# Giving each gathered block its own PSUM bank, from two pools by turns, and placing half of the shared expert behind the first gather

## The chip, the cores and the metric

The kernel runs on one core of a Trainium2 chip. The metric is the time of one execution on the device, in microseconds (us). Smaller is better. The core has a matrix engine (TensorE, PE in the rows, with its weight loads as PEld), a vector engine (VectorE, DVE), an activation engine (ScalarE, ACT), GpSimd (POOL) and SyncE (SP), which here only issues transfers from memory. [...]

## What is computed

One layer of a diffusion backbone over 256 latent tokens of width 1024. The first half (a recurrence, a neighbourhood attention, projections) is not touched by the change. The second half is a mixture of experts, and the change lies there:

```
scores = sigmoid(xb @ w_router)                      # 64 experts
sel = scores + router_bias                           # 4 of 8 groups, then the 8 best experts
w = scores[best] / sum(scores[best]) * 2.5
gates = sum(one_hot(best) * w)                       # token x expert
a = einsum('td,edf->tef', xb, w_e_gate)
u = einsum('td,edf->tef', xb, w_e_up)
act = silu(a) * u * gates
routed = einsum('tef,efd->td', act, w_e_down)
shared = (silu(xb @ w_sh_gate) * (xb @ w_sh_up)) @ w_sh_down
y2 = routed + shared
```

Each of the 64 experts has 3 MB of weights (gate and up 1 MB each, down 1 MB), read from memory once. The shared expert has the same shape and sees all tokens. Everything is in fp32, with some operands split in a high and a low part.

## The kernel before

**Routing.** After the first half, two tiles of 128 tokens (t = 0 and 1) are normalised, transposed on PE (L1194, from `x2` into tiles `pt`), scaled into `h2`, and multiplied with the router (L1204). `choose(t)` (L1159) finds the eight experts on DVE. Small products and DVE steps (L1222 to L1264) then rank the experts by load and give each token its place in its expert. PE's order in this stretch is not written out by hand: a scheduler at build time lists the instructions by readiness, earlier lines first, and takes the slots of a PSUM tag in the order in which the program asks for them.

**The shared expert.** `shared_gu(t, ks, after)` (L1470) multiplies the tokens of tile t with the shared gate and up weights: 16 matmuls for each t, which the trace counts as 32 records since an fp32 matmul is run in two. They read `h2` and the shared weights only. `after` names a PE instruction behind which the scheduler has to put them.

**Units.** The experts' work is cut into 29 units of up to 128 rows; each unit holds the tokens of one to four experts, in the order of `_ORDER` (L34). From L1488 on PE's order is written out, by `_program` (L53). For each unit u it is:

- `g`: `gate_up(u)` (L1393), the products with gate and up of the unit's experts into a `pgu` tile
- `s`: the first half of `scatter` (L1426) of unit u-1: two `py` products (t = 0 and 1), each added into `y` by DVE (L1432)
- `P`: `places(u+1)` (L1352): two transposes into `poh`, read twice by DVE (L1359, L1361); behind every second one `prepare` makes the one-hot matrix of the next pair of units on DVE
- `t`: `act_t(u)` (L1286): the activation on ACT, the product on DVE (L1294), two transposes `pat` on PE, a copy on ACT
- `S`: the second half of the scatter, two more `py` products
- `G`, in every second unit: `gather` (L1364) for the next pair of units
- `d`: `down(u)` (L1411), two `pdn` products, split by ACT (L1421) and DVE (L1422)

**The gather** makes the transposed tokens of a pair of units: for each of eight blocks k four matmuls (L1375) into PSUM, and then one instruction that scales the block into `xg`: on ACT for even k (L1378), on DVE for odd k (L1381). Blocks k and k+1 share one `pxg` tile, each in its half of the bank. The tool that builds the kernel orders all accesses of a PSUM tile by the bank and not by the bytes. The first gather (L1482) is called once before the units, is 128 columns wide and stands among the matmuls of `shared_gu`; the other fourteen stand in the units and are 256 columns wide.

**PSUM tags** (L1126 to L1136): `gu` has four banks, for `pgu` and for all tiles of `ps_y` (`py` and some of the routing); `mm` has two (`pxg`, `poh`, `pat`, and some of the routing); `dn` has two.

**Weights.** SP issues every load in the program's order (`fetch`, `fetch_ahead`, L258 and L294), each as soon as its slot in SBUF is free. There are six slots for gate and up and seven for down; a slot is freed when the last unit that uses its expert has run `g` or `d`. One of each is held by the shared expert at first. SP is in order, so a load that waits for its slot holds up those behind it.

Of the kernel before, what the change touches and what calls it, by code (L numbers as in the profile page):

```python
# [9 lines left out]
F32 = mybir.dt.float32  # L10
# [7 lines left out]
P = 128  # L18
D = 1024
T = 256  # L20
# [114 lines left out]
def build(ctx, tc, I, out, dbg=None):  # L135
    nc = tc.nc
# [6 lines left out]
    def pool(name, bufs=1, **kw):  # L143
        return ctx.enter_context(tc.tile_pool(name=name, bufs=bufs, **kw))
# [64 lines left out]
    def mpool(name, bufs=1, **kw):  # L209
        return mix.enter_context(tc.tile_pool(name=name, bufs=bufs, **kw))  # L210

    psum = mpool("psum", space=bass.MemoryType.PSUM)
# [902 lines left out]
    psum = pool("psum2", space=bass.MemoryType.PSUM)  # L1115
# [8 lines left out]
    fetch_ahead(False)  # L1124

    def ps_gu():  # L1126
        return psum.tile([P, 512], F32, tag="gu", name="pgu", bufs=4)

    def ps_mm(name):
        return psum.tile([P, 512], F32, tag="mm", name=name, bufs=2)  # L1130
# [1 line left out]
    def ps_dn():  # L1132
        return psum.tile([P, 512], F32, tag="dn", name="pdn", bufs=2)

    def ps_y():
        return psum.tile([P, 512], F32, tag="gu", name="py", bufs=4)  # L1136

    pb_ = route.enter_context(tc.tile_pool(name="pb", bufs=1))

# [3 lines left out]
    x2h = pkeep.tile([P, 2, KD, P], F32R, name="x2h")  # L1143
    x2l = pkeep.tile([P, 2, KD, P], F32R, name="x2l")
    y = x1
# [3 lines left out]
    on_pe, turned = [None, None], [None, None]  # L1149
# [39 lines left out]
    for t in range(2):  # L1189
        ts = slice(t * P, (t + 1) * P)  # L1190
        for kk in (0, 4):
            pt = ps_y() if t else ps_mm("pt")
            for i in range(4):
                turned[t] = nc.tensor.transpose(pt[:, i * P:(i + 1) * P], x2[:, t, kk + i, :], ident)  # L1194
            for i in range(4):
                k = kk + i
                if t and i % 2:
                    nc.vector.tensor_scalar(h2[k][:, ts], pt[:, i * P:(i + 1) * P], mod2[:, 1, k:k + 1],
                                            mod2[:, 0, k:k + 1], op0=OP.mult, op1=OP.add)
                else:  # L1200
                    on_act = nc.scalar.activation(h2[k][:, ts], pt[:, i * P:(i + 1) * P], AF.Identity,
                                                  bias=mod2[:, 0, k:k + 1], scale=mod2[:, 1, k:k + 1])
        for k in range(KD):
            on_pe[t] = nc.tensor.matmul(pl[:, t * NE:(t + 1) * NE], h2[k][:, ts], wr[:, k, :], start=(k == 0),  # L1204
                                        stop=(k == KD - 1))
        choose(t)
# [11 lines left out]


    pcn = ps_y()  # L1220
    for t in range(2):
        nc.tensor.matmul(pcn[:NE, 0:1], mask[:, t, :], ones[:, 0:1], start=(t == 0), stop=(t == 1))  # L1222
    pkr = ps_mm("pkr")
    for t in range(2):
# [14 lines left out]
    nc.vector.scalar_tensor_tensor(place, pp[:, 0:2 * NE].rearrange("p (t e) -> p t e", e=NE), 1.0, mask,  # L1239
                                   op0=OP.add, op1=OP.mult)  # L1240
    pix = ps_y()
    nc.tensor.matmul(pix[0:1, :NE], C("ecol")[:NE], R, start=True, stop=True)
    idx = pkeep.tile([1, NE], I32, name="idx")
# [61 lines left out]
    def prepare(pair):  # L1305

        us = [u for u in (2 * pair - 1, 2 * pair) if 0 <= u < len(units)]
        oh = pb2.tile([P, 2, 2 * P], F32R, tag="oh", name="oh", bufs=1)
        res = []
        for i, u in enumerate(us):  # L1310
            later = []
            used = 32 * sum(s[3] for s in units[u])
            if used < P:
                nc.vector.memset(oh[:, :, i * P + used:(i + 1) * P].bitcast(F32), 0.0)
            segs = list(units[u])
            while segs:
                j, s0, t0, n = segs[0]
                run = 1
                while run < len(segs) and segs[run][0] == j + run and segs[run][3] == n and not s0:
                    run += 1  # L1320
                segs = segs[run:]
                w_ = 32 * n
                a, b = 32 * t0, 32 * t0 + run * w_
                if run > 1:
                    sh4 = [P, 2, run, w_]
                    it = iota[:, None, None, 1:1 + w_].to_broadcast(sh4)
                    f4 = "p t (r c) -> p t r c"
                    nc.vector.tensor_tensor(oh[:, :, i * P + a:i * P + b].rearrange(f4, c=w_), it,
                                            pos[:, :, j:j + run, None].to_broadcast(sh4), op=OP.is_equal)
                else:  # L1330
                    for t in range(2):
                        nc.vector.tensor_scalar(oh[:, t, i * P + a:i * P + b], iota[:, s0 + 1:s0 + 1 + w_],
                                                pos[:, t, j:j + 1], None, op0=OP.is_equal)
                later.append((j, run, w_, a, b))
            res.append((u, i, used, later))
        return oh, res
# [27 lines left out]
    def gather(ohs_):  # L1364

        oh, res = ohs_
        w_ = len(res) * P
        xg = pb2.tile([P, KD, 2 * P], F32, tag="xg", name="xg", bufs=1)
        for k in range(KD):
            if k % 2 == 0:  # L1370
                pair_ = ps_mm("pxg")
            pg_ = pair_[:, k % 2 * T:k % 2 * T + w_]
            for t in range(2):
                for part in (x2h, x2l):
                    nc.tensor.matmul(pg_, part[:, t, k, :], oh[:, t, :w_],  # L1375
                                     start=(t == 0 and part is x2h), stop=(t == 1 and part is x2l))
            if k % 2 == 0:
                nc.scalar.activation(xg[:, k, :w_], pg_, AF.Identity, bias=mod2[:, 0, k:k + 1],  # L1378
                                     scale=mod2[:, 1, k:k + 1])
            else:  # L1380
                nc.vector.tensor_scalar(xg[:, k, :w_], pg_, mod2[:, 1, k:k + 1], mod2[:, 0, k:k + 1],  # L1381
                                        op0=OP.mult, op1=OP.add)
        for u, *_ in res:
            xgs[u] = xg

    def pieces(u):

        w_ = 32 * min(4 if n == 4 else 2 if n == 2 else 1 for *_, n in units[u])
        for j, _, t0, n in units[u]:
            for s in range(32 * t0, 32 * (t0 + n), w_):  # L1390
                yield j, s, w_

    def gate_up(u):  # L1393
        i = prep[u][0]
        xg = xgs.pop(u)
        o = ps_gu()
        for k in range(KD):
            for j, s, w_ in pieces(u):
                nc.tensor.matmul(o[s:s + w_], xg[:, k, i * P + s:i * P + s + w_], W["g"][j][:, :, k, :],  # L1399
                                 start=(k == 0), stop=(k == KD - 1))  # L1400
        return o
# [32 lines left out]
    def scatter_open(n, used, ohs, r_, _):  # L1434

        for t in range(2):
            pys[t, n] = py = ps_gu() if n else ps_y()
            for q, a in enumerate(r_[n]):
                nc.tensor.matmul(py, ohs[:used, t * P:(t + 1) * P], a[:used], start=(q == 0), stop=False,
                                 skip_group_check=True)  # L1440
# [25 lines left out]
    gu, dn = shw  # L1466

    pgs = [ps_gu(), ps_gu()]

    def shared_gu(t, ks, after):  # L1470
        with tc.issue_after(after):
            for k in ks:
                for q in range(2):
                    r = nc.tensor.matmul(pgs[t][:, q * FE:(q + 1) * FE], h2[k][:, t * P:(t + 1) * P], gu[:, q, k, :],  # L1474
                                         start=(k == 0 and q == 0), stop=(k == KD - 1 and q == 1),
                                         skip_group_check=True)
        return r.ins

    shared_gu(0, range(3), turned[0].ins)
    shared_gu(0, range(3, 8), turned[1].ins)  # L1480
    ohs_ = prepare(0)
    gather(ohs_)  # L1482
    shared_gu(1, range(8), on_pe[1].ins)
    free["g"].append(shs[0])
    fetch_ahead()

# [4 lines left out]
    for t in range(2):  # L1491
        for n in range(2):
            ns = slice(n * 512, (n + 1) * 512)
            py = ps_y()
# [6 lines left out]
    ohs_ = prepare(1)  # L1501
# [44 lines left out]
    for op, i in steps:  # L1546
        if op == "G":
            gather(ohs_)
        elif op == "P":
            places(ohg_)  # L1550
            if i % 2 == 0 and i < last_u:
                ohs_ = prepare(i // 2 + 1)
# [58 lines left out]
    with tc.If(nov > 0):  # L1611
# [3 lines left out]
        for k in range(KD):  # L1615
            px = ps_mm("px")
            for t in range(2):
                for part in (x2h, x2l):
                    nc.tensor.matmul(px[:, t * P:(t + 1) * P], part[:, t, k, :].bitcast(F32), ident,
                                     start=(part is x2h), stop=(part is x2l))  # L1620
            nc.vector.tensor_scalar(xa[:, k, :], px[:, :T], mod2[:, 1, k:k + 1], mod2[:, 0, k:k + 1],
                                    op0=OP.mult, op1=OP.add)
        with tc.For_i(0, NE, 1) as jv:
# [6 lines left out]
            for t in range(2):  # L1630
                o = ps_gu()
                for k in range(KD):
                    nc.tensor.matmul(o, xa[:, k, t * P:(t + 1) * P], ge[:, :, k, :], start=(k == 0),
                                     stop=(k == KD - 1))
                at = act_t(o, gl_[:, t, :])
                for n in range(2):
                    pd = ps_dn()
                    for jj in range(2):
                        nc.tensor.matmul(pd, at[:, jj, :], de[:, jj, n * 512:(n + 1) * 512], start=(jj == 0),
                                         stop=(jj == 1))  # L1640
# [34 lines left out]
```

## Time and profile before

| | |
|---|---|
| median of 3 runs | 1171.97 us (1171.61 to 1176.51) |
| the profiled execution: its own time | 1173.35 us |
| its span, first to last instruction | 1171.6 us |
| PE busy in the span | 1060.3 us (91%) |
| DVE busy | 678.0 us (58%) |
| ACT busy | 454.0 us (39%) |
| read from HBM | 293.05 MB |
| mean granted clock of PE | 0.964 |

The rows are of one execution. "Idle before, releaser" is the time that an engine stood still before an instruction, and what it waited for last. A busy PE is not a PE at its peak: ends of matmuls are modelled, so two starts tell more than a start and an end. [...] In the table by stretches the columns are the stretch, its length, busy us and instructions of PE, PEld, DVE, ACT and POOL, PEclk, the mean busy share of the DMA engines, and GB/s.

### The profile page before, as it was taken

The numbers are of one execution on the slowest core, as the hardware profiler recorded it, in microseconds if no ns is written. First come the engines' busy times: TensorE is split into PE (matmuls) and PEld (weight loads), VectorE is DVE, ScalarE is ACT, GpSimd is POOL, SyncE is SP. The second block draws the span as 40 slices with busy tenths as digits, with TensorE's granted clock in tenths as the row PEclk, the third lists the DMA queues.
The fourth block names the chain that finished last, engine by engine and source line by source line (L and its number), as shares of the span: only waits on it lengthen the run. The fifth ranks groups of instructions, "written<-read, shape, count | busy, mean of one in ns | idle before, by whom it ended". The sixth has DMA issues, their size and how long they took to land.

```text
span 1171.6 us, 18971 instructions
## 1 busy us (share of the span) xinstructions
PE 1060.3 (91%) x7232; PEld 744.9 (64%) x7232; DVE 678.0 (58%) x1323; ACT 454.0 (39%) x874; POOL 226.9 (19%) x215
## 2 busy tenths in 40 slices
PE   5998989999999989989988899899999999999995
PEld 3796968879898878779987544344434443444441
DVE  5587696958854868777784234343434434434355
ACT  4585847657644556556432011121111111211120
POOL 1126142343455537330010000000000000000021
PEclk9999989898999999999986989999999999999998
DMA  9945444534594434424975479999999999958991
GB/s 320 287 138 164 126 154 133 161 127 130 159 199 130 105 86 75 94 76 132 375 291 231 149 291 368 404 423 403 372 425 424 423 424 426 423 230 344 427 397 38
DMA packets 115101, 295.36 MB, mean 252 GB/s; under 512 B 7080, under 2 KB 86896, under 8 KB 90432
## 3 DMA queue, kind: packets, MB, share of 16 engines
q1 hardware_dynamic: 113088, 290.46, 65.8%
q0 software_dynamic: 1776, 3.47, 3.2%
q8 instruction: 58, 0.95, 0.3%
q14 instruction: 35, 0.29, 0.1%
q10 hardware_dynamic: 144, 0.20, 0.0%
HBM read 293.05 MB, written 1.05 MB: 251 GB/s over the span
## 4 chain that ended last, share of the span: by engine, by line
PE 53%; DVE 14%; DMA 9%; ACT 8%; issue 8%; POOL 5%; SPq 2%; DVEq 0%; ACTq 0%; POOLq 0%
PE pgu L1399 14%; PE proj L388 10%; PE pdn L1407 7%; PE pxg L1375 5%; PE py L1431 4%; DMA dn<-in_w_e_down_dram 3%; DVE wlo L336 3%; DMA wada<-in_w_ada_dram 2%; ACT xg L1378 2%; DMA G<-in_na_rpb_dram 2%; PE proj L394 2%; PE pgu L1474 1%; POOL kl L957 1%; DVE s L728 1%; DMA gu<-in_w_e_up_dram 1%
## 5 line engine op out<-in xcount | busy, mean ns | idle before, releaser
L1399 PE MATMUL pgu<-gu,xg 128*32 128x512 f32 (+1 forms) x1456 | 206.8, 593 | 3.4 <-DMA gu<-in_w_e_up_dram 1.8
L336 DVE TENSOR_TENSOR wlo<-wraw,whi 128x1024 fp32r<-128x1024 f32 x102 | 143.5, 1408 | 44.1 <-ACT whi L335 42.1
L1399 PEld LDWEIGHTS pgu<-gu,xg 128*32 128x32 f32 (+1 forms) x1456 | 65.4, 117 | 140.5 <-issue 129.2
L335 ACT CAST whi<-wraw 128x1024 fp32r<-128x1024 f32 x102 | 105.6, 1045 | 46.3 <-PE proj L388 35.5
L1294 DVE SCALAR_TENSOR_TENSOR ac<-ac,gcol,pgu 128x256 f32<-128x256 f32 (+1 forms) x29 | 13.9, 480 | 170.2 <-ACT ac L154 170.2
L1407 PE MATMUL pdn<-dn,at 128*32 128x512 f32 (+3 forms) x740 | 107.0, 595 | 0.0
L388 PE MATMUL proj<-hl,whi 128*128 128x256 f32 (+1 forms) x480 | 103.8, 331 | 0.0
L388 PE MATMUL proj<-hh,whi 128*128 128x256 f32 (+1 forms) x480 | 103.0, 333 | 0.0
L1375 PE MATMUL pxg<-oh,x2h 128*128 128x256 f32 (+1 forms) x240 | 68.6, 314 | 37.3 <-ACT xg L1378 36.9
L388 PE MATMUL proj<-hh,wlo 128*128 128x256 f32 (+1 forms) x480 | 101.1, 331 | 0.0
L1513 POOL TENSOR_TENSOR end<-cf,mod 128x1024 f32<-128x1024 f32 x1 | 1.9, 1898 | 497.8 <-DMA dn<-in_w_e_down_dram 497.8
L154 ACT ACTIVATE ac<-pgu 128x256 f32<-128x256 f32 (+1 forms) x31 | 11.9, 385 | 202.2 <-PE pgu L1399 192.3
L388 PEld LDWEIGHTS proj<-hh,wlo 128*128 128x128 f32 x480 | 77.0, 196 | 9.0 <-issue 1.4
L388 PEld LDWEIGHTS proj<-hh,whi 128*128 128x128 f32 x480 | 75.8, 196 | 7.0 <-issue 0.5
L388 PEld LDWEIGHTS proj<-hl,whi 128*128 128x128 f32 x480 | 74.8, 194 | 6.5 <-issue 0.7
L1375 PEld LDWEIGHTS pxg<-oh,x2h 128*128 128x128 f32 x240 | 46.5, 194 | 50.2 <-ACT xg L1378 48.7
L1421 ACT CAST rh<-pdn 128x512 fp32r<-128x512 f32 x56 | 32.8, 586 | 109.7 <-PE pdn L1407 94.8
L1381 DVE TENSOR_SCALAR xg<-pxg,mod 128x256 f32<-128x256 f32 (+1 forms) x60 | 32.0, 535 | 64.2 <-PE pxg L1375 63.5
L1432 DVE TENSOR_TENSOR x<-x,py 128x512 f32<-128x512 f32 x108 | 68.9, 679 | 0.0
L1422 DVE TENSOR_TENSOR rl<-pdn,rh 128x512 fp32r<-128x512 f32 x56 | 38.6, 691 | 51.2 <-ACT rh L1421 51.1
L601 ACT ACTIVATE wada<-wada,cond 128x256 f32<-128x256 f32 x128 | 58.6, 502 | 24.1 <-DMA wada<-in_w_ada_dram 24.1
L1407 PEld LDWEIGHTS pdn<-dn,at 128*32 128x32 f32 (+2 forms) x740 | 29.8, 117 | 58.9 <-issue 56.1
(389 smaller groups left out, 2057.3 us busy)
## 6 DMA issues: line engine op xcount, KB each, us to landing
gu<-in_w_e_gate_dram SPq DMA_DIRECT2D x64, 1024.0 KB, 12.3
gu<-in_w_e_up_dram SPq DMA_DIRECT2D x64, 1024.0 KB, 13.2
dn<-in_w_e_down_dram SPq DMA_DIRECT2D x61, 1024.0 KB, 13.4
wraw<-in_w_in_dram SPq DMA_DIRECT2D x80, 512.0 KB, 4.6
wada<-in_w_ada_dram SPq DMA_DIRECT2D x48, 512.0 KB, 4.6
wraw<-in_w_branch_a_dram SPq DMA_DIRECT2D x8, 512.0 KB, 3.5
wraw<-in_w_branch_b_dram SPq DMA_DIRECT2D x8, 512.0 KB, 3.9
wraw<-in_w_out_dram SPq DMA_DIRECT2D x8, 512.0 KB, 7.7
```

What stands on the lines that cost most here:

```text
L335: nc.scalar.copy(hi, raw)
L336: nc.vector.tensor_sub(lo, raw, hi.bitcast(F32))
L388: nc.tensor.matmul(o, a[:, m * P:(m + 1) * P], b[:, :n], start=first, stop=last)
L601: nc.scalar.activation(w, w, AF.Identity, scale=cond[:, k, 0:1])
L1375: nc.tensor.matmul(pg_, part[:, t, k, :], oh[:, t, :w_], start=(t == 0 and part is x2h), stop=(t == 1 and part is x2l))
L1381: nc.vector.tensor_scalar(xg[:, k, :w_], pg_, mod2[:, 1, k:k + 1], mod2[:, 0, k:k + 1], op0=OP.mult, op1=OP.add)
L1399: nc.tensor.matmul(o[s:s + w_], xg[:, k, i * P + s:i * P + s + w_], W["g"][j][:, :, k, :], start=(k == 0), stop=(k == KD - 1))
L1407: nc.tensor.matmul(pd[s:s + w_, :ns.stop - ns.start], at[:, jj, s:s + w_], W["d"][j][:, jj, ns], start=(jj == 0), stop=(jj == 1))
L1421: nc.scalar.copy(rh[:used], z)
L1422: last_rl[0] = nc.vector.tensor_sub(rl[:used], z, rh[:used].bitcast(F32)).ins
L1431: nc.tensor.matmul(py, ohs[:used, t * P:(t + 1) * P], a[:used], start=(q == 0), stop=(q == 1))
L1432: nc.vector.tensor_add(to[:, t, ns], to[:, t, ns], py)
```

## The change

`ps_y` gets a tag of its own, `y`, with two banks, and `gu` keeps two instead of four. The gather takes a new tile for every block k: k = 0, 1, 4, 5 from `mm` and k = 2, 3, 6, 7 from `y`. `gather` returns its last matmul, and `shared_gu(1, ...)` is put behind that one; before it was put behind the router's last matmul of tile 1.

```diff
     def ps_gu():
-        return psum.tile([P, 512], F32, tag="gu", name="pgu", bufs=4)
+        return psum.tile([P, 512], F32, tag="gu", name="pgu", bufs=2)
...
-    def ps_y():
-        return psum.tile([P, 512], F32, tag="gu", name="py", bufs=4)
+    def ps_y(name="py"):
+        return psum.tile([P, 512], F32, tag="y", name=name, bufs=2)
...
         for k in range(KD):
-            if k % 2 == 0:
-                pair_ = ps_mm("pxg")
-            pg_ = pair_[:, k % 2 * T:k % 2 * T + w_]
+            pg_ = (ps_y if k // 2 % 2 else ps_mm)("pxg")[:, :w_]
             for t in range(2):
                 for part in (x2h, x2l):
-                    nc.tensor.matmul(pg_, part[:, t, k, :], oh[:, t, :w_],
-                                     start=(t == 0 and part is x2h), stop=(t == 1 and part is x2l))
+                    r = nc.tensor.matmul(pg_, part[:, t, k, :], oh[:, t, :w_],
+                                         start=(t == 0 and part is x2h), stop=(t == 1 and part is x2l))
...
             xgs[u] = xg
+        return r.ins
...
-    gather(ohs_)
-    shared_gu(1, range(8), on_pe[1].ins)
+    shared_gu(1, range(8), gather(ohs_))
```

## Rows read from the trace of the kernel before

**Rows 1.** The span in 40 equal slices of 29.3 us: the granted clock of PE in tenths, and the busy share of the DMA engines in tenths.

```profile
PEclk9999989898999999999986989999999999999998
DMA  9945444534594434424975479999999999958991
```

**Rows 2.** Who waited for whom between 640 and 1160 us, the two rows of PE's matmuls that matter: us in total, times, longest.

```profile
PE pxg L1375 <- ACT xg L1378: 36.9, 57, 0.7
...
PE pgu L1399 <- DMA gu<-in_w_e_up_dram: 1.8, 1, 1.8
```

**Rows 3.** One gather in a unit, in order of time: start, length, engine, line, instruction.

```profile
744.86 0.28 PE L1375 MATMUL pxg<-oh,x2h 128*128 128x256 f32 x1
...
744.98 0.28 PE L1375 MATMUL pxg<-oh,x2l 128*128 128x256 f32 x1
...
745.53 0.57 ACT L1378 ACTIVATE xg<-pxg,mod 128x256 f32<-128x256 f32 x1 [1.03 <-PE pxg L1375]
...
746.15 0.39 PE L1375 MATMUL pxg<-oh,x2h 128*128 128x256 f32 x1 [0.66 <-ACT xg L1378]
...
747.00 0.54 DVE L1381 TENSOR_SCALAR xg<-pxg,mod 128x256 f32<-128x256 f32 x1 [0.15 <-PE pxg L1375]
...
751.74 0.38 PE L1375 MATMUL pxg<-oh,x2h 128*128 128x256 f32 x1 [0.66 <-ACT xg L1378]
...
752.20 0.28 PE L1375 MATMUL pxg<-oh,x2l 128*128 128x256 f32 x1
...
752.41 3.64 PE L1407 MATMUL pdn<-dn,at 128*32 128x512 f32 x32
```

**Rows 4.** The scatter just ahead of that gather, in order of time: DVE's product of the activation, its two sums of `s`, the two `py` products of `S` (each two matmuls), DVE's last reading of `poh`, and its two sums of `S`.

```profile
742.98 0.48 DVE L1294 SCALAR_TENSOR_TENSOR ac<-ac,gcol,pgu 128x256 f32<-128x256 f32 x1 [8.75 <-ACT ac L154]
...
743.38 1.28 DVE L1432 TENSOR_TENSOR x<-x,py 128x512 f32<-128x512 f32 x2
...
743.85 0.48 PE L1431 MATMUL py<-rh,ohs 128*128 128x512 f32 x1
...
744.39 0.40 PE L1431 MATMUL py<-rh,ohs 128*128 128x512 f32 x1
...
744.91 0.41 DVE L1361 TENSOR_SCALAR ohs<-poh 128x256 fp32r<-128x256 f32 x1
...
745.57 1.27 DVE L1432 TENSOR_TENSOR x<-x,py 128x512 f32<-128x512 f32 x2
```

**Rows 5.** The same two rows of the scatter in unit 27, the last of the 27 units that have a whole scatter.

```profile
1134.50 1.28 DVE L1432 TENSOR_TENSOR x<-x,py 128x512 f32<-128x512 f32 x2
...
1134.92 0.47 PE L1431 MATMUL py<-rh,ohs 128*128 128x512 f32 x1
```

**Rows 6.** The first gather in a unit: its first matmul and what follows it, in order of time.

```profile
671.45 0.37 PE L1375 MATMUL pxg<-oh,x2h 128*128 128x256 f32 x1
...
681.64 2.94 PE L1407 MATMUL pdn<-dn,at 128*32 128x512 f32 x16
```

**Rows 7.** The stretch from 673.5 to 683.7 us, in the table by stretches.

```profile
673.50:683.70 10.20, 8.23 (x37) 5.66 (x39) 3.35 (x11) 1.69 (x3) 0.00 (x0) 0.50 0.71 300
```

**Rows 8.** The routing and the first six us of the shared expert, in the table by stretches.

```profile
608.60:614.70 6.10, 3.75 (x17) 3.49 (x16) 5.29 (x8) 3.05 (x10) 0.55 (x2) 0.50 1.02 428
614.70:620.70 6.00, 5.64 (x25) 5.24 (x25) 4.60 (x25) 2.87 (x5) 0.00 (x0) 0.50 1.00 421
620.70:624.10 3.40, 1.71 (x9) 1.41 (x8) 2.65 (x21) 0.22 (x1) 0.00 (x0) 0.50 0.13 55
624.10:630.07 5.97, 5.04 (x20) 3.34 (x20) 3.22 (x17) 1.81 (x3) 0.00 (x0) 0.50 0.11 19
630.07:636.00 5.93, 5.93 (x15) 4.76 (x15) 0.79 (x3) 0.21 (x1) 0.00 (x0) 0.50 1.00 406
```

**Rows 9.** PE alone around the end of the routing, in order of time: the last `py` tile of the routing, the shared expert's tile 0, the first gather's first matmul, the end of tile 1.

```profile
629.03 1.11 PE L1263 MATMUL py<-R,tr 64*128 64x64 f32 x4 [0.46 <-ACT tr L1260]
630.07 10.06 PE L1474 MATMUL pgu<-gu,h 128*128 128x256 f32 x32
639.78 0.41 PE L1375 MATMUL pxg<-oh,x2h 128*128 128x128 f32 x1
...
645.56 5.83 PE L1474 MATMUL pgu<-gu,h 128*128 128x256 f32 x26
```

**Rows 10.** The units up to the last load, in the table by stretches: three parts, and the whole from 690 us on.

```profile
690.00:850.00 160.00, 145.84 (x1020) 66.44 (x1012) 65.38 (x144) 28.80 (x57) 0.00 (x0) 1.00 0.96 392
850.00:1015.00 165.00, 153.08 (x1004) 69.61 (x1005) 67.14 (x148) 29.54 (x59) 0.00 (x0) 1.00 1.01 424
1015.00:1065.00 50.00, 45.41 (x285) 21.82 (x284) 18.33 (x40) 9.17 (x18) 0.00 (x0) 1.00 0.67 273
690.00:1135.00 445.00, 408.86 (x2709) 188.76 (x2701) 179.43 (x391) 81.98 (x159) 9.09 (x5) 1.00 0.95 394
```

**Rows 11.** The products with gate and up of units 13 and 14 (counted from 0), in order of time; unit 14 is the one that holds three experts.

```profile
889.61 7.04 PE L1399 MATMUL pgu<-gu,xg 128*64 128x512 f32 x32
...
902.64 7.85 PE L1399 MATMUL pgu<-gu,xg 128*32 128x512 f32 x64
```

**Rows 12.** SP's issue of the last of the loads for that unit 14, and the time from issue to landing of the loads of gate and up issued between 876 and 886 us.

```profile
883.70 0.33 SPq L241 DMA_DIRECT2D gu<-in_w_e_up_dram  x1
...
DMA to landing us min/median/max: 19.6/19.7/19.7
```

## The prediction

> **What bounds the kernel now.** I read the slices first, then PE's waits in the units, then one gather in order of time, and last the loads, because whatever PE gains there has to be fed by them. In the slices PE is at its full clock from the 25th on, while the DMA engines are nearly full [rows 1]; from 690 us on the clock is 1.00 in every stretch [rows 10], so the clock has nothing to give back there. From 640 to 1160 us PE stands still for 36.9 us in front of gather matmuls, each time until ACT has read the block before, and only 1.8 us for a load [rows 2]. So the units are bound by PE, with one known hole in it, and the loads come in just ahead. How little ahead shows at unit 14: its last load was issued at 883.70 and took about 19.6 us, so it landed near 903.3, while PE began the unit at 902.64 and needed 7.85 us instead of 7.04 [rows 11, 12]. So whatever PE gains ahead of unit 14 must be gained by the loads too.
>
> **Part 1: a bank for each block.** Matmuls of a gather follow each other every 0.12 us [rows 3], so 32 of them are 3.74 us of work; the gather took from 744.86 to about 752.32, or 7.46. The difference is four stops of 0.93 us: the odd block of a pair writes the bank that ACT has yet to read (0.57 us), and PE stands until it has. With a bank for each block these stops go. What is late next is worked out on the same unit. Blocks 0 and 1 go to `mm`: one bank is free, the other when DVE has read `poh`, at 745.32, in time for block 1 [rows 4]. Blocks 2 and 3 go to `y`, whose banks hold the two `py` of `S` until DVE's sums end, at 746.25 and 746.85. The gather then starts at 745.23 (part 2), block 2 at 746.30 in place of 746.17, block 3 at about 746.9, and the other four find their banks read: DVE reads block 1 until 747.4, block 5 would write there at 747.8. The end is near 749.3, and `down` starts about 3.1 us sooner than its 752.41 [rows 3]. I take 3.0 (bounds: 2.0 if each of the blocks 4 to 7 also waits some 0.25 us for DVE; 3.35 with no wait), net of part 2 in the same unit. Thirteen gathers in units 2 to 26: **-39.0 us** (-26 to -43.5).
>
> [...]
>
> **Part 2: two banks for `py`.** The second half of a scatter starts at 743.85 and 744.39; its banks are now those of the first half, read by DVE until 744.06 and 744.66 (two sums in 1.28 us, from 743.38) [rows 4]. With 0.05 us for the signal the first `py` waits 0.26 us and the second leaves PE 0.32 us late; the same reckoning for unit 27 gives 0.37 [rows 5], and most of the 27 lie near that. Behind them on PE stand `G` or `d`. In the 13 units with a gather it is in the 3.0 already; in the 14 odd units it is a loss: 14 x 0.37 = **+5.2** (+4.5 to +12, the latter if the later sums slip by half a us too).
>
> **Part 3: the shared expert.** The matmuls of tile 0 take PE from 630.07 to 639.78, right behind the matmuls that write the routing's last `py` [rows 9]. They need only `h2` of tile 0 and weights that have long landed; PE had 5.3 us idle between 608.6 and 630.07 (21.47 less 16.14 busy) [rows 8], and none of it was used. The reason that fits is the tag: in `gu` their tile is asked for behind all the `py` of the routing, and slots are given in that order. In the new layout nothing stands ahead of it in `gu`, so the scheduler can put these matmuls into the gaps of the routing. The first gather then follows the routing directly, and tile 1's matmuls follow the gather; they are the same work, and their end releases the shared slot for the next load as before. At the lower clock of the routing [rows 8] a matmul record of this kind takes some 0.40 us (15 in 5.93), so 32 are 12.7 us; 5.3 go into gaps and up to 7.4 delay the routing, for a gain of 9.7 - 7.4 = 2.3. At the full clock they are about 7.0 us and the gain is up to 8.0. If the clock, which now rises in the dense stretch behind the routing, rises later instead, some 10 us of gather and tile 1 may run partly at the lower level and the gain turns into a loss of about 3. I take **-4** (-9.7 to +3), near the middle, because these are dense matmuls and may lift the clock sooner.
>
> **Part 4: the loads.** From 690 to 1135 us they move 394 GB/s x 445 us = 175 MB [rows 10]. At the 424 that the full stretch from 850 to 1015 shows, that is 413.5 us: the loads' end can move by at most 31.5 us, plus what their start moves (parts 3 and unit 0's gather: 4 + 4.6 = 8.6). The sum so far is 39.0 + 4.6 - 5.2 + 4 = 42.4 us, which is above these 40. The place where it binds is unit 14. Ahead of it PE gains 8.6 + 6 x 3.0 - 7 x 0.37 = 24.0 us; the loads gain 8.6 and, from 690 to 850, 160 - 392 x 160 / 424 = 12.1 us if no gap is left, 20.7 in all. So at least 3.3 us are lost there. Carrying the loads forward one by one (2.47 us for each MB behind another, a slot free when its last unit's `g` or `d` ends) leaves a few gaps between 690 and 750 and makes it 6 to 8, with 1 to 2 more about unit 25. I take **+6** (+3.3 to +14).
>
> **The sum.** -39.0 - 4.6 + 5.2 - 4 + 6 = -36.4 us. Against the profiled execution's own 1173.35 us that is 1137.0; the median of the runs is 1.4 us lower, so I forecast 1171.97 - 36.4, about **1136 us**.
>
> **The rivals.**
> - Tile 0 stays where it is, or what it gains the slower clock takes: then part 3 is 0 and the time 1140. For it: the clock stood at the lower level through the whole routing [rows 8]. Against it: the idle time and the tag.
> - The loads fill their gaps only half: 31.5 / 2 + 8.6 = 24.4 us of gain, 1148. For it: 273 GB/s from 1015 to 1065 [rows 10], where all slots wait for PE. Against it: that hole closes if PE is early.
> - The loads are already at the most that this memory gives over a long time, the mean of 394 [rows 10]: then only their earlier start is gained, 8.6 us, and the time is 1163. Against it: 424 over 165 us. [...]
> - All goes well: routing hides 8, unit 0's gather is at full clock, gathers gain 3.35, the loads cost 6: 43.6 + 6.5 + 8 - 5.2 - 6 = 46.9, about 1126.
> - Slower than before: the two banks of `y`. If the scheduler puts DVE's first sums behind the three readings and products for `poh` (1.2 us) and, in every second unit, behind the next pair's one-hot matrix (about 1.4 us), every scatter waits: 27 x 1.2 + 14 x 1.4 = 52 us against 36.4, so 1188. It decides from 36.4 / 27 = 1.35 us of added wait for each scatter. Against it: the sums stand right behind the activation's product in all rows [rows 4, 5].
> - The change doesn't do what it says, PE waiting for two banks of each pool as it did for halves: with two banks a block has about 1.4 us until its bank is asked for again, more than one reading (0.57), so this needs DVE late as above; 1172.
>
> **How the numbers follow.** Forecast 0.46 (its own range 1130 to 1143), tile 0 without gain 0.18, loads half 0.14, loads at their mean 0.04, all well 0.10, no change 0.03, slower 0.05. A change of 0.5% is about what a measurement of this kernel can tell; that is 6 us, so faster 0.92, same 0.03, slower 0.05. The range goes from 1124 (just past the good case) to 1150 (past the half-fed loads); outside it lie 0.04 + 0.03 + 0.05 and the tails.
>
> **What would show it.** Part 1: PE's wait for `xg` on ACT falls from 36.9 us to under 3, and a gather takes 4.0 to 4.4 us. Part 2: a new wait of PE's `py` on DVE's sums, some 8 to 10 us in 54 waits. Part 3: L1474 records between 609 and 630 us and the first gather's start before 637. Part 4: DMA at 424 GB/s through 700 to 850, PE waits for loads near units 12 to 14, 5 to 9 us in all, and a smaller hole about units 21 to 24. The forecast is wrong if gathers stay above 6 us, if scatter waits exceed 1 us each, or if PE's waits for loads pass 15 us.

## The result, and the profile after

The changed kernel takes **1141.98 us** (median of 4 runs, 1135.26 to 1143.22) against 1172.43 for the kernel before, a ratio of **0.9722** (95% interval 0.9678 to 0.9766): faster, by some 30 us, where 36 were forecast. The profiled execution's own time is 1142.01 us, its span 1140.1; against the 1173.35 of before that is 31.34 us.

First who waited for whom between 640 and 1160 us, which answers to [rows 2] (us in total, times, longest; PE for matmuls, PEld for their weight loads; rows of later work left out).

```profile
PE pgu L1398 <- DMA gu<-in_w_e_up_dram: 7.3, 4, 3.8
PEld py L1430 <- DVE x L1431: 6.8, 28, 0.3
PE py L1430 <- DVE x L1431: 4.2, 23, 0.3
PEld pgu L1398 <- DMA gu<-in_w_e_up_dram: 3.9, 2, 2.3
...
PEld pxg L1373 <- DVE x L1431: 2.9, 8, 1.6
PEld pgu L1398 <- DMA gu<-in_w_e_gate_dram: 2.4, 3, 0.8
...
PE pxg L1373 <- DVE x L1431: 1.4, 1, 1.4
```

The gather's 36.9 us of waits for ACT [rows 2] are gone. Two kinds are in their place: `py` on DVE's sums, 6.8 + 4.2 = 11.0 us in 51 short waits, and gate-up on loads, 7.3 + 3.9 + 2.4 = 13.6 us as the rows add up. PE's own matmuls stand for 7.3 of these, in four stops, and some rows of weight loads name the same stops again. Before, the same rows came to 1.8 [rows 2] and 1.6:

```profile
PEld pgu L1399 <- DMA gu<-in_w_e_gate_dram: 1.6, 2, 0.8
```

In the rows of after the last, a stop of 1.4 us for DVE's sums, is in the gather of unit 26.

One gather with the second half of the scatter ahead of it, in order of time, which answers to [rows 3, 4].

```profile
728.41 1.28 DVE L1431 TENSOR_TENSOR x<-x,py 128x512 f32<-128x512 f32 x2
...
728.52 0.38 PE L1357 MATMUL poh<-cf,ohg 128*128 128x128 f32 x2
729.24 0.47 PE L1430 MATMUL py<-rh,ohs 128*128 128x512 f32 x1
...
729.75 0.19 PEld L1430 LDWEIGHTS py<-rh,ohs 128*128 128x128 f32 x1 [0.24 <-DVE x L1431]
...
730.31 0.28 PE L1373 MATMUL pxg<-oh,x2h 128*128 128x256 f32 x1
...
731.80 0.54 DVE L1379 TENSOR_SCALAR xg<-pxg,mod 128x256 f32<-128x256 f32 x1
...
734.05 0.28 PE L1373 MATMUL pxg<-oh,x2l 128*128 128x256 f32 x1
...
734.50 1.92 PE L1406 MATMUL pdn<-dn,at 128*32 128x512 f32 x16
```

From 730.31 to `down` at 734.50 the gather takes 4.2 us, without a stop; before, it took 7.62 us to the end of its last matmul in each of the units 2 to 24. Ahead of it `py` stands 0.24 us for DVE, as the sums of the first half are read out until 729.69.

The stretches that answer to [rows 10] (columns as there: length, PE, PEld, DVE, ACT, POOL, PE's granted clock as a share of full speed, DMA share, GB/s).

```profile
690.00:850.00 160.00, 155.49 (x1100) 69.34 (x1098) 68.23 (x151) 30.54 (x60) 0.00 (x0) 1.00 1.00 417
850.00:1015.00 165.00, 159.44 (x956) 71.83 (x954) 68.29 (x151) 30.54 (x60) 0.00 (x0) 0.98 0.99 417
1015.00:1065.00 50.00, 49.42 (x408) 22.89 (x404) 21.34 (x45) 10.29 (x20) 0.00 (x0) 1.00 0.89 362
```

The DMA engines are now full from 690 us on (their share is 1.00 and 0.99 up to 1015), but for a shorter pause: it is 0.32 from 1010 to 1020, where before it was 0.16 over the 15 us from 1030 to 1045. Unit 14, where the prediction had placed the bind [rows 11, 12], looks like this: PE in order of time, and the clock through it.

```profile
878.31 2.14 PE L1398 MATMUL pgu<-gu,xg 128*32 128x512 f32 x6
884.29 9.53 PE L1398 MATMUL pgu<-gu,xg 128*32 128x512 f32 x58 [3.85 <-DMA gu<-in_w_e_up_dram]
```

```profile
881.00:885.00 4.00, 0.71 (x4) 0.23 (x8) 0.00 (x0) 0.00 (x0) 0.00 (x0) 0.69 1.01 426
885.00:890.00 5.00, 5.00 (x32) 1.42 (x28) 0.00 (x0) 0.00 (x0) 0.00 (x0) 0.57 1.03 434
890.00:894.00 4.00, 4.00 (x31) 1.15 (x24) 0.00 (x0) 0.14 (x1) 0.00 (x0) 1.00 1.01 414
```

The unit's products with gate and up take from 878.31 to 893.82, 15.51 us in place of 7.85. After the stop the clock is at 0.57 for 5 us, which costs, by an estimate from these rows, 5 x 0.43 = 2.2 us on top of the wait.

**The routing.** The stretches of after that answer to [rows 7 to 9].

```profile
612.00:616.00 4.00, 4.00 (x16) 3.55 (x14) 2.66 (x5) 0.09 (x1) 0.55 (x1) 0.50 1.02 430
616.00:624.00 8.00, 8.00 (x55) 7.14 (x54) 5.62 (x35) 3.19 (x7) 0.00 (x0) 0.98 0.75 313
624.00:630.00 6.00, 4.37 (x27) 2.94 (x27) 4.95 (x28) 1.17 (x3) 0.00 (x0) 0.99 0.00 0
630.00:640.00 10.00, 10.00 (x42) 9.34 (x42) 3.81 (x13) 3.06 (x6) 0.00 (x0) 0.50 0.93 362
640.00:646.00 6.00, 6.00 (x29) 5.07 (x27) 0.00 (x0) 0.00 (x0) 0.00 (x0) 0.99 0.24 100
```

Tile 0's shared matmuls now stand between 610 and 626 us, and PE is full there at a clock that rises, from 0.50 before 616 us to 0.98 behind it; the first gather starts at 630.36 instead of 639.78. But tile 0 is used up by 626, PE idles 1.6 us between 624 and 630, and the clock is at 0.50 for the next 10 us. There lie the first gather (7.09 us; before it took 5.95 at a clock of 1.00, with six records of tile 1 among its own) and the first 2.75 us of tile 1:

```profile
630.36 0.47 PE L1373 MATMUL pxg<-oh,x2h 128*128 128x128 f32 x1
...
637.25 8.56 PE L1473 MATMUL pgu<-gu,h 128*128 128x256 f32 x32
...
656.34 2.03 PE L1398 MATMUL pgu<-gu,xg 128*32 128x512 f32 x16 [1.41 <-issue]
```

**Where the 31.34 us lie.** I cut every execution at four places of PE's timeline: the first transpose of the routing (L1194), the first gate-up matmul of unit 0, of unit 1 and of unit 28, and the end of the profiled execution.

| us | start of the routing | to unit 0 | to unit 1 | to unit 28 | to the end | own time |
|---|---|---|---|---|---|---|
| before | 607.59 | 54.51 | 24.02 | 453.49 | 33.74 | 1173.35 |
| after | 608.27 | 48.07 | 17.10 | 434.73 | 33.84 | 1142.01 |
| difference | +0.68 | -6.44 | -6.92 | -18.76 | +0.10 | -31.34 |

### The profile page after: what moved, and what is told of

It reads as the page before. It is cut to its first block, busy times and chain, and to the rows that moved or that the text cites. A ratio compares the mean times of both kernels' runs of the same rounds, so it can differ in the third digit from the quotient of the medians.

```text
span 1140.1 us, 18936 instructions
## 1 busy us (share of the span) xinstructions
PE 1054.8 (93%) x7232; PEld 735.9 (65%) x7232; DVE 678.0 (59%) x1323; ACT 453.5 (40%) x874; POOL 226.7 (20%) x215
## 4 chain that ended last, share of the span: by engine, by line
PE 48%; DVE 15%; DMA 14%; issue 8%; ACT 6%; POOL 5%; SPq 2%; DVEq 0%; ACTq 0%; POOLq 0%
PE pgu L1398 14%; PE proj L388 10%; PE pdn L1406 6%; DMA gu<-in_w_e_up_dram 5%; PE pxg L1373 4%; DMA gu<-in_w_e_gate_dram 3%; DVE wlo L336 3%; DMA wada<-in_w_ada_dram 3%; DMA G<-in_na_rpb_dram 2%; PE proj L394 2%; PE py L1430 2%; DVE s L728 2%; POOL kl L957 2%; PE pgu L1473 1%; SPq L319 1%
## 5 line engine op out<-in xcount | busy, mean ns | idle before, releaser
L1398 PE MATMUL pgu<-gu,xg 128*32 128x512 f32 (+1 forms) x1456 | 211.7, 601 | 8.8 <-DMA gu<-in_w_e_up_dram 7.3
L1373 PE MATMUL pxg<-oh,x2h 128*128 128x256 f32 (+1 forms) x240 | 64.1, 302 | 1.4 <-DVE x L1431 1.4
L607 POOL TENSOR_TENSOR wada<-wada 128x1024 f32<-128x1024 f32 x16 | 44.3, 2769 | 97.4 <-ACT wada L601 83.4
L1373 PE MATMUL pxg<-oh,x2l 128*128 128x256 f32 (+1 forms) x240 | 61.3, 289 | 0.0
```

Source lines behind the costliest of these rows:

```text
L607: nc.gpsimd.tensor_tensor(w0, w0, w1, op=OP.add)
L1373: r = nc.tensor.matmul(pg_, part[:, t, k, :], oh[:, t, :w_], start=(t == 0 and part is x2h), stop=(t == 1 and part is x2l))
```

## The experiments

The theory: the gather's stops went as forecast, the pools put tile 0 into the routing, and the loads took back more than the 6 us that the sum gave them. The rivals: the scatter's two banks took it, or where tile 1 now stands. Each ratio below is against the kernel before, timed on the same chip. For each run here are the times between the same cuts, in us; "light" is a kernel with fewer bytes to load.

| | to unit 0 | to unit 1 | to unit 28 |
|---|---|---|---|
| pools alone | 40.87 | 20.47 | 464.86 |
| tile 1 back | 39.31 | 17.11 | 432.28 |
| four shared banks | 52.85 | 17.08 | 426.74 |
| third `py` from `gu` | 47.98 | 17.10 | 433.06 |
| light, after | 46.19 | 17.10 | 422.91 |
| light, before | 53.67 | 25.57 | 454.58 |
| unit moved | 48.10 | 17.10 | 425.69 |
| tile 1 back, unit moved | 39.69 | 17.10 | 425.47 |
| filler, unit moved | 44.55 | 17.10 | 425.24 |
| all three | 40.48 | 18.63 | 425.08 |
| after, once more | 47.99 | 17.11 | 432.27 |

**The pools alone** (the kernel before, two banks for each tag):

```diff
-        return psum.tile([P, 512], F32, tag="gu", name="pgu", bufs=4)
+        return psum.tile([P, 512], F32, tag="gu", name="pgu", bufs=2)
...
-        return psum.tile([P, 512], F32, tag="gu", name="py", bufs=4)
+        return psum.tile([P, 512], F32, tag="y", name="py", bufs=2)
```

> The kernel before with one edit: py from two banks of its own, pgu from two. The gather and the place of tile 1 stay as they were. Theory: the tag order is what held tile 0's shared matmuls, so they now run between 609 and 630 us and unit 0 starts some 6 us earlier; each scatter waits about 0.5 us for its banks, in 27 units 13 us; the gathers keep their stops (36.9 us). Time 1172 - 6 + 13 = 1179 us. Rival 1: in units with a gather the scatter's wait is hidden in the gather's own stops, so only 14 x 0.47 = 6.6 us are lost, 1172 us. Rival 2: tile 0 doesn't gain anything by the pools, 1185 us.

Measured: 1169.76 us, ratio 0.9984 (0.9959 to 1.0009), no difference that can be told. The theory's sum was 9 us off, but not by the scatter: that cost was 464.86 us from unit 1 to unit 28 against 453.49, 11.4 us or 0.42 in each of 27 units, so rival 1 (hidden in the units with a gather) falls. What was off is the start. From the first transpose to unit 0 it takes 40.87 us, not 54.51: **13.6 us** less, twice the 6 that the whole change shows. In its list of PE's instructions tile 0 stands in the routing's gaps and, behind it, 7 of tile 1's 16 matmuls too; the clock is 1.00 from 612 us on, through the whole stretch. Rival 2 falls. The first transpose, the first of tile 0's matmuls, and the first matmul of unit 0:

```profile
605.26 1.09 PE L1194 MATMUL pt<-cf,x 128*128 128x128 f32 x8 [2.46 <-ACT x L1186]
...
606.99 1.17 PE L1474 MATMUL pgu<-gu,h 128*128 128x256 f32 x2
...
646.13 2.46 PE L1399 MATMUL pgu<-gu,xg 128*32 128x512 f32 x20 [1.41 <-issue]
```

**Banks and pools as in the change, tile 1 back where it was:**

```diff
-    shared_gu(1, range(8), gather(ohs_))
+    gather(ohs_)
+    shared_gu(1, range(8), on_pe[1].ins)
```

> The changed kernel with shared_gu(1) put back behind the router's last matmul of tile 1. Theory: what the routing gained comes from the pools and not from where tile 1 stands, and the loads bind at unit 14 whatever PE gains ahead of it, so the time stays within 5 us of the changed kernel, 1137 to 1146 us; part of tile 1's matmuls now fills routing gaps too, and the first gather starts at most 2 us from where it did. Rival: the place of tile 1 brought the 6 us at the start, and they go, 1148 us.

Measured: 1133.59 us, ratio 0.968 (0.9641 to 0.9719), below what theory and rival had named. It takes 39.31 us to unit 0, 8.8 less than the changed kernel. So the third edit of the change, tile 1 behind the first gather, *loses* 8 to 9 us on the way to unit 0, and the pools alone had brought the whole gain at the start. In the whole time the two intervals overlap; the same edit with the unit moved, below, shows it there as well. Its stretches show why: PE has no gap and the clock no fall, and the first gather takes 3.79 us.

```profile
620.00:632.00 12.00, 12.00 (x76) 9.68 (x74) 8.68 (x51) 2.67 (x7) 0.00 (x0) 1.00 0.39 164
632.00:640.00 8.00, 8.00 (x55) 7.30 (x53) 3.65 (x13) 2.72 (x6) 0.00 (x0) 1.00 0.93 368
```

**No separate bank pool for `py`, gathers still one block to a bank:**

```diff
     def ps_gu():
-        return psum.tile([P, 512], F32, tag="gu", name="pgu", bufs=2)
+        return psum.tile([P, 512], F32, tag="gu", name="pgu", bufs=4)
...
-        return psum.tile([P, 512], F32, tag="y", name=name, bufs=2)
+        return psum.tile([P, 512], F32, tag="gu", name=name, bufs=4)
```

> The changed kernel with pgu, py and the gather's second pool in one tag of four banks again. Theory: no scatter waits for a bank (about 0.5 us less in each of 27 units, 13 us of PE's time), gathers stay at 4.3 us, and tile 0's shared matmuls stand behind the routing again (6 us later into unit 0); as the loads bind up to unit 14 and start later, the time is 1140 to 1146 us, with longer waits for loads than in the changed kernel. Rival 1: PE alone sets the time, 1142 + 6 - 13 = 1135 us. Rival 2: the scatter waits are DVE being late and not the banks, so they stay and the time is 1148 us.

Measured: 1138.71 us, ratio 0.974 (0.9699 to 0.9782), between theory and rival 1. No wait of `py` on DVE is left among PE's waits, and two units (unit 5 to unit 7) take 30.18 us in place of 31.12: 0.94, or 0.47 for each scatter, is the price of the two banks; rival 2 falls. In the list of PE's instructions tile 0 stands behind the routing again, as the order of the tag says it must, and unit 0 comes 52.85 us after the first transpose, 4.8 later than in the changed kernel. From unit 1 to unit 28 it takes 426.74 us, 8.0 less than the changed kernel: PE gained 13.5 pairs x 0.94 = 12.7, and the rest came back mostly as waits for loads in units 11 to 14 and 25:

```profile
PE pgu L1398 <- DMA gu<-in_w_e_up_dram: 9.0, 4, 3.9
...
PEld pgu L1398 <- DMA gu<-in_w_e_up_dram: 4.1, 2, 3.8
```

**The third `py` from `gu`,** whose second bank is idle then:

```diff
-            py = ps_y()
+            py = ps_gu() if n and not t else ps_y()
```

> The changed kernel with the third py of each scatter taken from the gu tag, whose second bank is idle at that moment. Theory: the third and fourth py no longer wait for the first two sums (PE's waits for py on DVE fall from 11 us to under 3), PE could gain 27 x 0.45 = 12 us, but the loads take most of it back: waits for loads grow from 13.6 to over 20 us and the time is 1134 to 1139 us. Rival 1: PE sets the time, 1142 - 12 = 1130 us or less. Rival 2: the loads take all of it, 1142 us.

Measured: 1139.06 us, ratio 0.9726 (0.9686 to 0.9765): not to be told from the changed kernel. The waits of `py` on DVE are gone, as expected, but the rows of the waits for loads did not grow (7.9 + 2.8 = 10.7 us). By the times of the units that stop for loads (4, 12, 14 and 25, against a neighbour that does not) the loads took 2.4 us more than in the changed kernel, which is no more than the two profiles of that kernel differ by. The gather took most of the gain: it comes sooner, and a block then waits for ACT. A gather takes 5.06 us in place of 4.3. The row of the waits, and one such wait in order of time:

```profile
PE pxg L1373 <- ACT xg L1376: 8.5, 13, 0.7
```

```profile
731.41 0.38 PE L1373 MATMUL pxg<-oh,x2h 128*128 128x256 f32 x1 [0.66 <-ACT xg L1376]
```

So theory and rivals all missed where most of it went.

**Fewer bytes, same work for PE,** for the changed kernel and for the kernel before:

```diff
-    def load_dn(d_ap, slot, start=start, ns=slice(0, D)):
+    def load_dn(d_ap, slot, start=start, ns=slice(0, D), nj=2):
...
-        start(dn[:, :, ns], d_ap[..., ns].rearrange("o (p j) d -> (o p) j d", j=2))
+        start(dn[:, :nj, ns], d_ap[..., ns].rearrange("o (p j) d -> (o p) j d", j=2)[:, :nj])
...
-            W[op][j] = load_dn(wed[e], slot, start, CUT[0] if j in final else slice(0, D))
+            W[op][j] = load_dn(wed[e], slot, start, CUT[0] if j in final else slice(0, D),
+                              2 if j in final else 1)
...
-                nc.tensor.matmul(pd[s:s + w_, :ns.stop - ns.start], at[:, jj, s:s + w_], W["d"][j][:, jj, ns],
+                nc.tensor.matmul(pd[s:s + w_, :ns.stop - ns.start], at[:, jj, s:s + w_], W["d"][j][:, jj if j in final else 0, ns],
```

Both leave out half of the routed experts' down weights, so what they compute is not the layer; they serve for times alone.

> The changed kernel with only half of each routed expert's down weights read from memory, except for the last unit's (2.5 MB for each expert in place of 3); the products with them read the first half twice, so PE has the same work. Theory: PE stands for loads for some 14 us in the changed kernel's units 4, 12, 14 and 26, and that goes: 1128 us, 1125 to 1131. Rival: the stops in units 12 and 14 have another cause than the amount of the loads, 1140 us or more.

> The kernel before with the same cut of the down weights. Theory: there the loads kept ahead of PE but for some 3 us in units 4 and 14, so 1168 to 1171 us, and between this kernel and the changed one with the same cut lies what the change does for PE alone, some 41 us. Rival: the loads held PE up before as well, in ways that the waits don't show, 1160 us or less.

Measured: 1128.01 us, ratio 0.9618 (0.958 to 0.9655), for the first, and 1174.86, ratio 1.0002 (0.997 to 1.0033), for the second. The theory's 1128 is met. Between the two medians lie 46.85 us, where 41 were named for PE alone. The kernel before gains nothing that can be told, not even the 3 us of its few waits, so the forecast for it missed: loads were no bound there, and with the change they are. In the light changed kernel the long stops are gone, the scatter's waits are as they were, and the DMA engines are no longer full (its lines are one further down in the program):

```profile
PEld py L1431 <- DVE x L1432: 6.8, 28, 0.3
...
PE pgu L1399 <- DMA gu<-in_w_e_up_dram: 1.2, 1, 1.2
```

```profile
690.00:850.00 160.00, 157.13 (x1111) 70.36 (x1108) 68.89 (x153) 31.00 (x61) 0.00 (x0) 1.00 0.93 365
850.00:1015.00 165.00, 163.10 (x1036) 76.57 (x1038) 74.99 (x167) 33.82 (x66) 0.00 (x0) 1.00 0.86 343
```

From unit 1 to unit 28 the light changed kernel takes 422.91 us. So the loads cost the changed kernel 434.73 - 422.91 = **11.8 us**, and the PE side of the change in these units is 453.49 - 422.91 = **30.6 us**. From light kernel to light kernel it is 454.58 - 422.91 = 31.7. The loads' cost varies from one execution to another: by the second profile of the changed kernel, at the end of this section, it is 432.27 - 422.91 = 9.4.

**A unit moved in the order,** the changed kernel otherwise:

```diff
-_ORDER = [..., [0, 41], [20, 42, 43], [8, 44], ..., [3, 49], [27, 28], [29, 30], ...]
+_ORDER = [..., [0, 41], [8, 44], ..., [3, 49], [27, 28], [20, 42, 43], [29, 30], ...]
```

> The changed kernel with one unit of three experts, [20, 42, 43], moved in the order from the 10th place to behind [27, 28], so that less has to be loaded ahead of units 12 to 14. Theory: their waits for loads go (11 us with the slower clock behind the stop), 3 to 5 us of new waits come in units 17 to 26, and part of the loads' pause between 1004 and 1018 us is filled: 1132 to 1137 us. Rival: the loads have a total that can't be moved, and the waits only change their place, 1142 us.

Measured: 1132.71 us, ratio 0.9673 (0.9642 to 0.9704), 9 us below the changed kernel's median (7 below that of its later timing, 1139.76), as forecast, though the two intervals still touch. No unit about 850 stops any more, the clock is 1.00 throughout, the loads' pause is filled, and the time from unit 1 to unit 28 falls to 425.69 us. Of the new waits that were expected some 2.7 us came, in unit 25.

```profile
850.00:1015.00 165.00, 163.05 (x1071) 76.71 (x1070) 74.78 (x166) 33.56 (x66) 0.00 (x0) 1.00 1.01 424
1015.00:1065.00 50.00, 47.92 (x382) 19.88 (x375) 20.28 (x46) 9.21 (x18) 0.00 (x0) 1.00 1.01 420
690.00:1100.00 410.00, 401.23 (x2650) 182.84 (x2649) 179.68 (x392) 80.27 (x156) 9.11 (x5) 1.00 1.01 420
```

**Both: tile 1 back and the unit moved** (the two diffs together).

> Both: tile 1's shared matmuls back behind the router's last matmul of tile 1, and the unit moved. Theory: the first gives unit 0 some 8 us sooner than in the changed kernel, since the clock stays at its full level through the routing, the loads start as much sooner, and the second takes the waits of units 12 to 14: 1123 to 1129 us. Rival: the two gains overlap in the loads' total, 1133 us, as with tile 1 put back alone.

Measured: 1124.67 us, ratio 0.9599 (0.9566 to 0.9631), as the theory had it, and below the interval of the unit moved alone, on the same chip. To unit 0 it takes 39.69 us, 8.4 less than with tile 1 behind the gather (48.10), and from unit 1 to unit 28 425.47, the same. This beats both kernels.

**Filler.** What of these 8.4 us is the clock, and what the matmuls that leave the path? The changed kernel with the unit moved, plus 8 matmuls (16 records) of tile 1 made once more for nothing:

```diff
+    shared_gu(1, range(4), on_pe[1].ins)
     shared_gu(1, range(8), gather(ohs_))
```

> The changed kernel with the unit moved, as before, and tile 1 behind the first gather, but with the first 8 of its 16 shared matmuls made once more behind the router's last matmul of tile 1, for nothing: they stand where tile 1's own stand when it is put back (its products over those blocks are made twice). Theory: PE's idle stretches in the routing are what drops the clock, so with the filler it stays at 1.00 up to 645 us, the first gather takes 3.8 us in place of 7.1 and tile 1 about 7.0 in place of 8.6; unit 0 starts some 4 to 5 us sooner than with the unit moved alone, 1127 to 1130 us. Rival 1: the whole gain of putting tile 1 back is that its matmuls leave the path behind the gather; the filler then gives nothing, 1133 us. Rival 2: the clock is all of it, 1125 us.

Measured: 1128.7 us, ratio 0.9618 (0.958 to 0.9656), as the theory had it. To unit 0 it takes 44.55 us, 3.5 less than without the filler (48.10), though PE has more to do: the clock does not fall, and the first gather takes 3.87 us instead of 7.09.

```profile
624.00:635.00 11.00, 11.00 (x75) 9.23 (x74) 6.84 (x33) 4.19 (x8) 0.00 (x0) 1.00 0.34 127
635.00:642.00 7.00, 7.00 (x34) 6.05 (x33) 1.40 (x6) 0.03 (x1) 0.00 (x0) 1.00 0.96 403
```

The filler has a cost of its own: the first gather starts 23.19 us after the first transpose, 1.1 later than without it. So the clock is worth 3.5 us after that cost is paid, or 4.6 with the cost added back, and the other 3.8 to 4.9 are the matmuls that ran in gaps; both rivals, all of the one or all of the other, fall.

**The best order with the third `py` from `gu`.**

> Tile 1 put back, the unit moved, and the third py of each scatter from the gu tag. Theory: the loads are now the bound from 690 us on, so the 2 to 3 us that this takes from PE's units come back as waits for loads: no change against the version without it, 1123 to 1127 us. Rival: PE still sets the time, 1121 us or less.

Measured: 1123.2 us, ratio 0.9569 (0.9531 to 0.9606), which can't be told from the version without it. From unit 1 to unit 28: 425.08 us against 425.47. This is as the theory says, but it does not test it well, since the gathers of this kernel take 5.07 us here too and PE has little to give.

**The changed kernel once more,** unedited.

> The changed kernel itself, beside the two others on the same chip. Theory: 1139 to 1143 us, its clock at the lower level behind 629 us and about 10 us lost by loads in units 12 and 14. Rival: the fall of the clock behind 629 us belongs to one execution and not to the program, and it is missing here; then unit 0 starts some 4 us sooner and the time is near 1136 us.

Measured: 1139.76 us, ratio 0.9715 (0.9679 to 0.9752). To unit 0 it takes 47.99 us, the first gather 7.09, and from unit 1 to unit 28 432.27, 2.5 less than in the first profile. The rival falls: the fall of the clock belongs to this order of PE's work. All five profiles of it (two pools, tile 1 wholly behind the gather, no filler) have the first gather at 7.09 us; in the four with the gaps filled, by tile 1 or by the filler, it took 3.79 to 3.87.

## Why the prediction came out as it did

The forecast was 36.4 us of gain; the profiled execution shows 31.34. By the prediction's own terms:

| term | forecast | measured | from |
|---|---|---|---|
| parts 1 and 2, units 1 to 28 | -33.8 | -30.6 | before less the light changed kernel |
| unit 0's gather | -4.6 | -6.9 | unit 0 to unit 1 |
| part 3 | -4 | -6.4 | first transpose to unit 0 |
| part 4 | +6 | +11.8 | changed kernel less the light one |
| start of the routing and tail | 0 | +0.8 | table of the result |
| sum | -36.4 | -31.3 | |

That the sum is only 5 us off is in part luck: two terms came out 4.7 us better than forecast, the others 9.8 worse. The time alone would fit the rival without a gain of tile 0 (1140) as well as the forecast (1136); only the cuts and the runs tell them apart.

**Part 1** was right: the stops go, and the gather takes 4.25 to 4.34 us where 4.0 to 4.4 were named (in unit 26 5.73, with its stop for DVE). A unit with a gather gains 2.84 us (unit 6 to unit 7: 20.50 us before, 17.66 after), not 3.0. **Part 2** was right in kind and small in size: a unit without a gather loses 0.49 us (unit 7 to unit 8: 12.95 to 13.44), not 0.37, and the sum of the waits is 11.0 us where 8 to 10 were named. The run with four shared banks shows the same price, 0.47 for each scatter, with and without a gather behind it. The two together are the 3.2 us short.

**Unit 0's gather** stands in the sum with -4.6 and in the rival where all goes well with 6.5; these were the author's estimates, and no run shows them. In their place the runs show 6.9 us less from unit 0 to unit 1. Before, the gather took 10.26 us [rows 6], with the clock at 0.50 from 673.5 to 683.7 us [rows 7]; after, it took 4.34, with the clock at 1.00. That is 5.9 of the 6.9 us; the rest is `down`, whose first 2.06 us also stood at 0.50 before.

**Part 3** came out near its number for reasons that the number did not hold. The tag argument is shown: four banks in one tag put tile 0 behind the routing, two and two put it into the gaps, with the rest of the code unchanged. But the step said of tile 1's matmuls that "they are the same work", and gave their new place no price. It has one: with tile 1 free to follow tile 0, 7 of its 16 matmuls fill the gaps that tile 0 leaves, which the change forbids. Of 13.6 us that the pools alone win at the start, the changed kernel keeps 6.4. The loss that the prediction named, the clock that "rises later", is there, in another way: it rises early, at 616, and falls again at 630.

**Part 4** is the term that was mis-sized most, 11.8 us (9.4 by the second profile) within its bounds of 3.3 to 14. The place was right: against the light kernel 2.5 us are lost in unit 12 (9.62 less 7.09), 8.4 in unit 14 (15.51 less 7.07) and 0.7 ahead of unit 26. Three things were off in the reckoning. It had worked out 6 to 8 at unit 14 and 1 to 2 about unit 25, 7 to 10 in all, and took 6. It let PE come 24.0 us sooner to unit 14, and its loads at most 20.7; PE would have come 26.8 sooner (902.64 - 878.31 = 24.3, and the 2.5 lost in unit 12), since the start gained more than was forecast, but the unit's last load was issued only 19.2 us sooner, at 864.54 in place of 883.70 [rows 12]:

```profile
864.54 0.33 SPq L241 DMA_DIRECT2D gu<-in_w_e_up_dram  x1
```

From 690 to 850 the loads ran at 417 GB/s and not at the bound's 424, which is 160 x 7 / 424 = 2.6 us. So 7.6 us were missing there in place of the bound's 3.3. And it knew no price of a stop beyond the stop; the clock behind it made some 2.2 us more. 7.6 + 2.2 + 0.7 = 10.5 of the 11.8.

Of the **rivals**, the loads at their mean of 394 GB/s are out: with the unit moved they ran at 420 over the 410 us from 690 to 1100. Loads that fill their gaps only half are out too: from 690 to 850 the share of the DMA engines was 1.00, at 417 GB/s. DVE did not come late to the sums: no wait of `py` is above 0.3 us.

**What would have been a better version** follows from the same terms: keep the pools and the banks, leave tile 1 where it was, and spread the loads' demand by moving one unit. That is the kernel of 1124.67 us.

## What to carry to other kernels

When a change has several edits, price each alone, also the one that looks like a mere change of place: here two edits won some 39 us between them and the third gave 8 back, since tile 1's matmuls were worth more in the gaps of the routing's small dependent steps than behind them (39.31 us to unit 0 against 48.07). When the engine that bounds a kernel gets faster by some per cent, carry the loads forward to each unit, and allow for a stop to cost more than its wait (here, by the estimate from the clock of 0.57 behind it, some 2.2 us more for a stop of 3.85). A bank taken from one user to speed another has a price at each use; 0.47 us at 27 places was nearly a third of the 43 us that the gathers won (13 x 3.3).

## What the hardware showed that was not expected

In the changed kernel the granted clock fell from 0.99 to 0.50 behind a stretch in which PE was busy 4.37 of 6.00 us, and stayed down for 10 us in which PE was busy all the time; in the run with the filler, whose dummy matmuls filled that stretch (11.00 of 11.00 us busy), it was 1.00. It also fell behind a wait in the midst of the units, to 0.57 for 5 us after 4 us with 0.71 us busy. So the stretch in which PE was not full cost more than its 1.63 us of idle time: matmuls that compute nothing shortened the way to unit 0 by 3.5 us. What exactly lowers the clock stays open: in the same execution PE was busy only 2.74 of 4.00 us a little later, and the clock stayed at 1.00.

```profile
646.00:650.00 4.00, 2.74 (x11) 1.52 (x11) 2.37 (x8) 1.03 (x3) 0.00 (x0) 1.00 0.76 264
650.00:656.00 6.00, 4.93 (x14) 1.92 (x12) 2.52 (x5) 0.00 (x0) 0.00 (x0) 1.00 0.51 186
```
